# Value products four units behind instead of three, five tiles of transposed probabilities instead of four, and each group's output stored right behind its last eviction

## The chip, the core and the metric

The kernel runs on one core of a Trainium2 chip. Its engines each work through their own instructions in order and wait for one another through semaphores: TensorE (PE) multiplies, VectorE (DVE), ScalarE (ACT) and GpSimd (POOL) work on tiles, and SyncE (SP) and ScalarE issue the DMA transfers. The metric is the device time of one execution in microseconds, the median of the runs. In what follows PEld is TensorE's weight load, and "ACTq" and "SPq" are the sequencers of ScalarE and SyncE, which issue DMAs.

## The reference, cut to what matters

One layer of an encoder over 4096 tokens of width 1024. A single projection feeds two halves: a gated convolution of width 3, and attention with 8 heads of 64. Attention is a band of 64 neighbours to each side, taken three times, over tokens at distance 1, 4 and 16, and the three results are mixed by their log-sum-exp:

```python
for window, dilation in ((128, 1), (512, 4), (2048, 16)):
    logits = einsum(q, k) * dh ** -0.5 + bias        # 128 queries by 256 keys at a time
    m = max(logits); p = exp(logits - m); denom = sum(p)
    o = einsum(p, v) / denom;  lse = m + log(denom)
mix = softmax(stack(lses));  o = sum(mix * outs)
x = x + einsum(concat(y_conv, o * silu(z_attn)), w_out)
```

## The kernel before, in words

The program has three stages. The first projects every token to queries, keys, values and gate and writes them to DRAM (up to about 740 us of the profile). The second, from 740 to 1834 us, interleaves two streams of work on every engine: the attention, and the dense matmuls of the convolution half (L854 to L856, `fill`). The third, from 1834 us to the end, joins the three attention results and applies the output projection, a tile of 128 tokens at a time. The order of every engine's instructions is the order in which the Python code emits them; no scheduler moves them.

The attention is cut into 384 **units**. A unit is 128 queries by up to 256 keys for a pair of heads. Eight units with the same heads, dilation and place are a **group**, so there are 48 groups; below, b is a unit's place in its group (0 to 7). A unit u goes through these steps:

- `qk` (L1044, L1045): the logits on TensorE; `logits` (L1057): bias and row maximum on VectorE, written into a tile `L`, the maximum into the group's output tile `ot`; `exps` (L1066): the exponential on ScalarE, in place.
- `p_hi` and `p_lo`: the probabilities as two half-precision parts, by ScalarE and then VectorE. For a unit with u % 3 == 1, TensorE first transposes the probabilities (`tr_pe`, L1086), and `p_hi` (L1092) and `p_lo` (L1104) write the two parts into a tile `pt`. For the other two of three, `p_hi` (L1098) and `p_lo` (L1108) write them untransposed into one of three tiles `src`, and a DMA transposition issued by SP (`tr`, L1112) brings them into `pt`.
- `av` (L1123 to L1125): twelve small matmuls of `pt` with the values `vt`; ScalarE evicts the product into `ot` (L1126).

The loop over units (L1162 to L1209) emits, in iteration u: `p_hi(u)`, `p_lo(u)`, `exps(u+1)`, `tr(u)`, half of the iteration's dense matmuls, `av(u - LAG)`, `qk(u+2)`, `logits(u+2)`, the group's transfers, the other half of the dense matmuls, and `tr_pe(u+1)` where u+1 is of that kind. So `LAG` says how many units the value products are behind the probabilities, and `PTB`, the number of `pt` tiles, is one more than that.

The group's transfers are issued on ScalarE's queue. The store of the group before (`o_store`, L1137 to L1141: one DMA of 528 KB, or two of 264 KB where the dilation is 16) and the load of the values of the next group (`load_v`, L935 to L952: three, four or, for the first and last groups of dilation 1, eight DMAs) each have their place by b. There are two `ot` tiles, so `logits` of the first unit of a group (emitted two iterations ahead, at b = 6 of the group before) may write only when the store of the group two before has landed.

The rings of tiles share one SBUF budget. `WB` is the number of staging tiles `wst` (128 x 512 float, 2 KB a partition, as a `pt` tile) in the second and third stage. They take the bias tables, and near the end of the second stage the output weights, which ScalarE's queue loads (L138) and `split` (L131 on ScalarE, L134 on VectorE or GpSimd) cuts into two parts; each of these loads is emitted two background steps behind the split of the tile three loads before it.

Of the kernel before, what the change touches and what calls it, by code (L numbers as in the profile page):

```python
# [46 lines left out]
BIG = 3.0e38  # L47
VEC = 383
CJ = (0, 2, 3, 1)
PTB = 4  # L50
CHUNKS = ((0, 1024, 71, 1), (1024, 2048, 79, 1), (2048, 3072, 87, 1), (3072, 4096, 94, 2))
SRCB = 3
LB = 3
WA = 3
WB = 4
WD = 12
LAG = 3
QZB = 4


# [5 lines left out]
def tile_hybrid_block(  # L66
# [581 lines left out]
    phB = ExitStack()  # L648
    stage[0] = phB.enter_context(tc.tile_pool(name="stageB", bufs=WB))
    pb = phB.enter_context(tc.tile_pool(name="pb", bufs=1))  # L650
# [60 lines left out]
    def c_room4():  # L711
        M["res", 1] = pb.tile([128, 1024], F32, name="bt")
        M["ja1"] = pb.tile([128, 512], F32, name="bt0")
# [12 lines left out]
    def sz_load(t):  # L726
        nc.sync.dma_start(M["sz", t % 3], sz_d[t * 128:(t + 1) * 128])
# [39 lines left out]
    def y_planes(t):  # L767
        halves = M["ja0", t % 2].bitcast(U16).rearrange("p (c b) -> p b c", b=2)
        src = pb.tile([128, 2, 512], U16, name="L", bufs=LB)
        YA[t] = pb.tile([128, 2, 4, 128], U16, name="pt", bufs=PTB)  # L770
        nc.vector.tensor_copy(src[:, 0], halves[:, 0])
# [186 lines left out]
    for gi, (pr, g, grp) in enumerate(groups):  # L958
        d = DILS[g]
        for b in range(8):  # L960
# [8 lines left out]
            U = dict(pr=pr, g=g, d=d, grp=grp, gi=gi, b=b, vidx=vidx, kn=256, c0=0)  # L969
# [92 lines left out]
    def exps(u):  # L1062
        U = units[u]
        ot, b, L = OT[U["gi"]], U["b"], ST[u]
        for i in range(2):
            nc.scalar.activation(L[:, i], L[:, i], AF.Exp, scale=-1.0,  # L1066
                                 bias=ot[:, b, i, DH:DH + 1], accum_out=ot[:, b, i, DH + 1:DH + 2])
# [3 lines left out]
    def by_pe(u):  # L1071
        return u % 3 == 1

    def src_of(u):
        return SRC[(u - (u + 1) // 3) % SRCB]
# [12 lines left out]
    def p_hi(u):  # L1088
        U = units[u]
        if by_pe(u):  # L1090
            PT[u] = pb.tile([128, 2, 2, 2, 128], F16, name="pt", bufs=PTB)
            nc.scalar.activation(PT[u][:, 0].rearrange("p a b q -> p (a b) q"), ST[u], AF.Copy, scale=P_SCALE)  # L1092
            return
        src = src_of(u)
        c = slice(U["c0"], U["c0"] + U["kn"])
        if U["kn"] < 256:
            nc.gpsimd.memset(src.rearrange("p a b c -> p (a b) c")[:, :, dead(U)], 0.0)
        nc.scalar.activation(src[:, 0, :, c], ST[u], AF.Copy, scale=P_SCALE)  # L1098

    def p_lo(u):  # L1100
        U = units[u]
        if by_pe(u):
            hi, lo = (PT[u][:, n].rearrange("p a b q -> p (a b) q") for n in range(2))
            nc.vector.scalar_tensor_tensor(lo, ST.pop(u), P_SCALE, hi, op0=OP.mult, op1=OP.subtract)  # L1104
            return
        c = slice(U["c0"], U["c0"] + U["kn"])
        src = src_of(u)
        nc.vector.scalar_tensor_tensor(src[:, 1, :, c], ST.pop(u), P_SCALE, src[:, 0, :, c], op0=OP.mult, op1=OP.subtract)  # L1108

    def tr(u):  # L1110
        PT[u] = pb.tile([128, 2, 2, 2, 128], F16, name="pt", bufs=PTB)
        nc.sync.dma_start(PT[u].rearrange("p a b c q -> p (a b c) q"), src_of(u).rearrange("p a b c -> p (a b c)"), transpose=True)  # L1112
# [49 lines left out]
    for u in range(NU):  # L1162
        U = units[u]
        p_hi(u)
        p_lo(u)
        if u + 1 < NU:
            exps(u + 1)
        if not by_pe(u):
            tr(u)
        fill(pers[u] / 2)  # L1170
        if u >= LAG:
            av(u - LAG)
        if u + QZB + 2 < NU and units[u + QZB + 2]["d"] == 1 and units[u + QZB + 2]["b"] % 2 == 0:
            q_order(u + QZB + 2)
        if u + QZB + 1 < NU:
            q_alone(u + QZB + 1)
        if u + 6 < NU:
            k_dense(u + 6)
        if u + 2 < NU:
            qk(u + 2)  # L1180
        if u + 3 == NU:
            c_room2()
            sz_load(0)
        if u + 2 < NU:
            logits(u + 2)
        if u + 3 == NU:
            c_room4()
        if u > 8 and U["b"] == LAG + 1:
            o_store(U["gi"] - 1)
        if U["b"] == LAG and U["gi"] + 1 < len(groups):  # L1190
            VT[U["gi"] + 1] = load_v(*groups[U["gi"] + 1])
        fill(pers[u] / 2)
        if u + 1 < NU and by_pe(u + 1):
            tr_pe(u + 1)
        if state["done"]:
            for _ in range(4):
                if bg:
                    bg.pop(0)()
        pr = U["pr"]
        if u == 4:  # L1200
            load_bias(0, 0)
            load_bias(0, 1)
        for a, b, at, rate in CHUNKS:
            p, n = divmod(u - at, 96)
            for n in range(rate * n, min(5, rate * n + rate) if 0 <= p < 3 else 0):
                load_stacks(p + 1, n, a, b)
        n = u - LAG
        if n > 0 and n % 32 == 0 and n // 32 <= 9:
            load_bias((n - 32) // 96 + 1, order[0][(n // 32 - 1) % 3])  # L1209
# [7 lines left out]
    list(conv_half(2, 0))  # L1217
    for u in range(NU - LAG, NU):
        av(u)
# [97 lines left out]
```

## Time and profile before

| | |
|---|---|
| median of 3 runs | 2181.21 us |
| lowest and highest | 2176.76 and 2185.51 us |
| the profiled execution's own time | 2186.28 us |
| its span, first to last instruction | 2184.5 us |
| PE busy | 2081.3 us, 95% |
| DVE, ACT, POOL busy | 66%, 49%, 39% |
| mean granted TensorE clock | 0.987 |

The page of the profile has a line for each group of instructions, with the busy time, the mean of one, and the idle time of the engine just before them with what ended it. The view of waits gives for each pair "engine line <- what it waited for" the sum in us, the number of waits and the longest. A timeline row has the start in us, the duration, the engine, line, operation and tiles, and in brackets the idle time before it and what ended that. A row of a windows view has for each engine the busy time and in parentheses the number of instructions, then the granted TensorE clock, the busy share of the DMA engines, and what they moved in GB/s.

### The profile page before, as it was taken

What the parts mean: (1) busy time and instruction counts of PE and PEld (TensorE: products, weight loads), DVE (VectorE), ACT (ScalarE), POOL (GpSimd) and SP (SyncE); (2) the same over time, 40 slices, a digit from 0 to 9 for tenths busy, and PEclk for the clock granted to TensorE, in tenths of its full rate; (3) what the DMA queues carried; (4) which work ended last, traced back from release to release, by engine and by line L of the source; (5) the groups of instructions that cost most, each with busy time, mean ns of one, the idle gap of its engine ahead of it and who ended that gap; (6) DMA issues with size and microseconds to landing.
All of it is one profiled execution on the core that took longest, in us unless ns stands there. A gap on an engine that the chain in (4) does not pass through costs nothing. (4 is left out here: it accounts for less than half of the span.)

```text
span 2184.5 us, 48540 instructions
## 1 busy us (share of the span) xinstructions
PE 2081.3 (95%) x17462; PEld 1533.7 (70%) x17462; DVE 1441.1 (66%) x4032; ACT 1069.4 (49%) x3095; POOL 851.8 (39%) x1635
## 2 busy tenths in 40 slices
PE   7699999999999989998999999999999999999999
PEld 3244444444444778888888888888888887788887
DVE  7755666656665366766677656675667676887776
ACT  6323333433432167666677656666667674222221
POOL 0322232332323265433554346433453454343332
PEclk9899999999999999999999999999999999999999
DMA  5255489975554877799877998769977687787775
GB/s 204 88 153 174 142 176 172 221 177 161 169 169 137 179 138 164 147 164 186 164 160 137 172 194 136 153 120 176 204 141 129 122 171 225 233 256 244 244 244 183
DMA packets 692397, 378.34 MB, mean 173 GB/s; under 512 B 470721, under 2 KB 636732, under 8 KB 688060
## 3 DMA queue, kind: packets, MB, share of 16 engines
q1 hardware_dynamic: 570788, 304.72, 62.0%
q10 hardware_dynamic: 121368, 70.53, 13.7%
q8 instruction: 137, 2.24, 0.4%
q14 instruction: 104, 0.85, 0.1%
HBM read 157.77 MB, written 110.39 MB: 123 GB/s over the span
## 5 line engine op out<-in xcount | busy, mean ns | idle before, releaser
L854 PE MATMUL bank<-hb,w 128*128 128x256 f16 x2048 | 560.9, 274 | 0.3 <-ACT cu L861 0.3
L856 PE MATMUL bank<-hb,w 128*128 128x256 f16 x2048 | 560.8, 274 | 0.0
L855 PE MATMUL bank<-hb,w 128*128 128x256 f16 x2048 | 560.8, 274 | 0.0
L410 PE MATMUL bank<-wa,hb 128*128 128x512 f16 x1024 | 391.4, 382 | 14.9 <-DMA hb<-xs 11.4
L1057 DVE CUSTOM_DVE_ANT_0 L<-bank,bt,alpha 128x256 f32<-128x256 f32 (+1 forms) x768 | 319.0, 453 | 126.3 <-PE bank L1045 74.1
L1066 ACT ACTIVATE L<-L,ot 128x256 f32<-128x256 f32 (+1 forms) x768 | 364.2, 476 | 60.0 <-DVE ot L1057 58.4
L412 PE MATMUL bank<-wa,hb 128*128 128x512 f16 x1024 | 391.2, 382 | 0.8 <-DMA hb<-xs 0.7
L411 PE MATMUL bank<-wa,hb 128*128 128x512 f16 x1024 | 390.9, 382 | 0.3 <-DVE wa L301 0.2
L1018 POOL COPY qz<-qk 64x128 f16<-64x128 f16 x512 | 163.9, 320 | 152.9 <-PE bank L1045 134.6
L1108 DVE SCALAR_TENSOR_TENSOR src<-L,src 128x512 f16<-128x512 f32 (+1 forms) x256 | 171.3, 669 | 71.6 <-ACT src L1098 67.5
L856 PEld LDWEIGHTS <-w 128*128 128x128 f16 x2048 | 201.2, 98 | 24.0
L855 PEld LDWEIGHTS <-w 128*128 128x128 f16 x2048 | 201.2, 98 | 22.8 <-issue 0.5
L854 PEld LDWEIGHTS <-w 128*128 128x128 f16 x2048 | 201.3, 98 | 20.7
L238 POOL TENSOR_TENSOR rs_rq<-rs_mq,mhalf 128x8 f32<-128x8 f32 x64 | 104.9, 1639 | 268.4 <-DVE rs_mq L237 261.4
L410 PEld LDWEIGHTS <-hb 128*128 128x128 f16 x1024 | 101.6, 99 | 136.4 <-DMA hb<-xs 13.8
L1123 PE MATMUL bank<-vt,pt 128*128 128x64 f16 x1536 | 176.6, 194 | 18.9 <-DMA pt<-src 16.3
L412 PEld LDWEIGHTS <-hb 128*128 128x128 f16 x1024 | 100.6, 98 | 125.3 <-issue 4.4
L411 PEld LDWEIGHTS <-hb 128*128 128x128 f16 x1024 | 100.8, 98 | 123.5 <-issue 5.5
L1125 PE MATMUL bank<-vt,pt 128*128 128x64 f16 x1536 | 176.6, 194 | 0.0
L1124 PE MATMUL bank<-vt,pt 128*128 128x64 f16 x1536 | 176.5, 194 | 0.0
L1098 ACT ACTIVATE src<-L 128x512 f16<-128x512 f32 (+1 forms) x256 | 148.4, 580 | 52.4 <-issue 25.2
L441 ACT ACTIVATE h<-wk 128x512 f16<-128x512 f32 x64 | 40.3, 630 | 257.2 <-DVE wk L437 152.3
(211 smaller groups left out, 4440.1 us busy)
## 6 DMA issues: line engine op xcount, KB each, us to landing
o_d<-ot ACTq DMA_DIRECT2D x32, 528.0 KB, 6.1
qk<-o_d SPq DMA_DIRECT2D x63, 264.0 KB, 4.4
hT<-hb SPq DMA_DIRECT2D x16, 1024.0 KB, 4.1
wst<-in_w_in_dram SPq DMA_DIRECT2D x64, 256.0 KB, 3.2
hb<-hT SPq DMA_DIRECT2D x16, 1024.0 KB, 6.4
qk<-in_x_dram SPq DMA_DIRECT2D x32, 512.0 KB, 5.5
qk_d<-h SPq DMA_DIRECT2D x128, 96.0 KB, 2.1
vt<-v_d ACTq DMA_DIRECT2D x48, 256.0 KB, 5.8
```

The costliest lines, as they stand in the source:

```text
L410: nc.tensor.matmul(p, hi[:, kt, :], w[:, 0], start=kt == 0, stop=False)
L411: nc.tensor.matmul(p, hi[:, kt, :], w[:, 1], start=False, stop=False)
L412: nc.tensor.matmul(p, lo[:, kt, :], w[:, 0], start=False, stop=kt == KT - 1)
L854: nc.tensor.matmul(pt, w_h, hi[:, :, kt], start=kt == 0, stop=False)
L855: nc.tensor.matmul(pt, w_h, lo[:, :, kt], start=False, stop=False)
L856: nc.tensor.matmul(pt, w_l, hi[:, :, kt], start=False, stop=kt == KT - 1)
L1057: nc.vector.tensor_tensor_reduce(out=L[:, i], in0=p[i][:, 0:kn], in1=bias[:, U["b0"]:U["b0"] + kn], scale=alpha, scalar=BIG, op0=OP.add, o ...
L1066: nc.scalar.activation(L[:, i], L[:, i], AF.Exp, scale=-1.0, bias=ot[:, b, i, DH:DH + 1], accum_out=ot[:, b, i, DH + 1:DH + 2])
L1108: nc.vector.scalar_tensor_tensor(src[:, 1, :, c], ST.pop(u), P_SCALE, src[:, 0, :, c], op0=OP.mult, op1=OP.subtract)
L1123: nc.tensor.matmul(p[:, i], hi, v[:, 0:DH], start=j == 0, stop=False)
L1124: nc.tensor.matmul(p[:, i], hi, v[:, DH:], start=False, stop=False)
L1125: nc.tensor.matmul(p[:, i], lo, v[:, 0:DH], start=False, stop=j == 1)
```

## The change

Four constants and one condition. `LAG` goes from 3 to 4 and `PTB` from 4 to 5; the added `pt` tile takes the room of one staging tile, `WB` going from 4 to 3. The last `av` of a group stands in the iteration with b == LAG - 1 of the next group, which was b = 2 and is now b = 3. The store of that group stood at b == LAG + 1 (4), two iterations later; it now stands at b == LAG - 1 (3), in the same iteration as that last `av`, right behind it. `load_v`, emitted at b == LAG, moves from 3 to 4. The reload of the bias tables goes by u - LAG and so comes one unit later, too.

```diff
-PTB = 4
+PTB = 5
@@
-WB = 4
+WB = 3
 WD = 12
-LAG = 3
+LAG = 4
@@
-        if u > 8 and U["b"] == LAG + 1:
+        if u > 8 and U["b"] == LAG - 1:
             o_store(U["gi"] - 1)
         if U["b"] == LAG and U["gi"] + 1 < len(groups):
             VT[U["gi"] + 1] = load_v(*groups[U["gi"] + 1])
```

TensorE's order at the first place that differs, iteration 3 of the loop (the rows with - are those before; L854 to L856 are dense matmuls, L1123 to L1125 `av` of unit 0, of which the first three of twelve matmuls are shown):

```order
 L856 LDWEIGHTS w_6133
 L856 MATMUL bank_7137<-hb_6257,w_6133 128x256
-L1123 LDWEIGHTS pt
-L1123 MATMUL bank_7194<-vt,pt 128x64
-L1124 LDWEIGHTS pt
-L1124 MATMUL bank_7194<-vt,pt 128x64
-L1125 LDWEIGHTS pt
-L1125 MATMUL bank_7194<-vt,pt 128x64
```

The value products of unit 0 leave iteration 3 for iteration 4, at the same place in the iteration, and so on for every unit; the last four units' products stand behind the loop, where there were three.

ScalarE's order around the group's transfers, units 179 and 180 (b = 3 and 4 of the group numbered 22, of dilation 4). L1098 is `p_hi`, L1066 `exps`, L1126 the eviction of `av`, L939 to L943 `load_v`, L1139 `o_store`, L861 an eviction of the dense matmuls. Before:

```order
L1098 ACTIVATE src_6576<-L 128x512 [waits Activation_49]
L1066 ACTIVATE L,ot<-L,ot 128x256 [waits DVE_49] x2
L1126 ACTIVATE ot<-bank_16469 128x2x64 [waits PE_49]
L939 DMA vt<-v_d 64x8x256 [waits DMAHW4_49]
L940 DMA vt<-v_d 64x8x256 [waits DMAHW6_49]
L942 DMA vt<-v_d 64x256 [waits DMAHW7_49]
L943 DMA vt<-v_d 64x256 [waits DMAHW0_49]
L861 ACTIVATE cu<-bank_16440,inv 128x256 [waits PE_49]
L1098 ACTIVATE src_6574<-L 128x512 [waits Activation_49,Pool_49]
L1066 ACTIVATE L,ot<-L,ot 128x256 [waits DVE_49] x2
L1126 ACTIVATE ot<-bank_16526 128x2x64 [waits PE_49]
L1139 DMA o_d_83<-ot 128x8x132 [waits DMAHW2_49]
```

With the change:

```order
L1098 ACTIVATE src_6576<-L 128x512 [waits DMAHW3_49,Activation_49]
L1066 ACTIVATE L,ot<-L,ot 128x256 [waits DVE_49] x2
L1126 ACTIVATE ot<-bank_16455 128x2x64 [waits PE_49]
L1139 DMA o_d_83<-ot 128x8x132 [waits Activation_49]
L861 ACTIVATE cu<-bank_16426,inv 128x256 [waits PE_49]
L1098 ACTIVATE src_6574<-L 128x512 [waits DMAHW6_49,Pool_49]
L1066 ACTIVATE L,ot<-L,ot 128x256 [waits DVE_49] x2
L1126 ACTIVATE ot<-bank_16508 128x2x64 [waits PE_49]
L939 DMA vt<-v_d 64x8x256 [waits DMAHW7_49,DMAHW4_49]
L940 DMA vt<-v_d 64x8x256 [waits DMAHW0_49]
L942 DMA vt<-v_d 64x256 [waits DMAHW1_49]
L943 DMA vt<-v_d 64x256 [waits DMAHW2_49]
```

The store comes one iteration earlier and ahead of the value loads instead of behind them, and it waits for ScalarE's own eviction (Activation) right in front of it; the value loads come one iteration later.

ScalarE's order where the output weights are loaded and split, near the end of the second stage. L138 is the load of a staging tile, L131 ScalarE's part of a split. Before:

```order
L131 ACTIVATE w_26655<-wst 128x512 [waits DMAHW2_49]
L824 DMA y_d<-cc 128x257 [waits Pool_49]
L1126 ACTIVATE ot<-bank_26666 128x2x64 [waits PE_49]
L138 DMA wst<-in_w_out_dram 128x512 [waits DMAHW0_49,Activation_49]
L131 ACTIVATE w_26699<-wst 128x512 [waits DMAHW3_49]
L1092 ACTIVATE pt<-bank_26707 128x512 [waits PE_49]
```

With the change:

```order
L131 ACTIVATE w_26641<-wst 128x512 [waits DMAHW2_49]
L824 DMA y_d<-cc 128x257 [waits Pool_49]
L1126 ACTIVATE ot<-bank_26652 128x2x64 [waits PE_49]
L138 DMA wst<-in_w_out_dram 128x512 [waits DMAHW0_49,Pool_49]
L131 ACTIVATE w_26685<-wst 128x512 [waits DMAHW3_49]
L1092 ACTIVATE pt<-bank_26693 128x512 [waits PE_49]
```

The order is the same, but the load goes into the tile that the split just before it reads, so it now waits for GpSimd's part of that split (Pool), which before belonged to a tile one load further back.

## The prediction

> **What bounds the kernel now.** I read the page first, then TensorE's groups with the idle time before each, then stretches of the second stage, and last the timeline around single waits.
>
> ```profile
> span 2184.5 us, 48540 instructions
> PE 2081.3 (95%) x17462; PEld 1533.7 (70%) x17462; DVE 1441.1 (66%) x4032; ACT 1069.4 (49%) x3095; POOL 851.8 (39%) x1635
> ...
> L1123 PE MATMUL bank<-vt,pt 128*128 128x64 f16 x1536 | 176.6, 194 | 18.9 <-DMA pt<-src 16.3 <-ACT ct L866 1.6 <-ACT ot L1126 0.9
> L1086 PE MATMUL bank<-identf,L 128*128 128x128 f32 x512 | 88.2, 283 | 32.3 <-ACT L L1066 22.9 <-POOL L L1053 8.0
> ```
>
> TensorE is busy 95% of the span, and the change takes no matmul from it, so only its idle time can be won. The second stage, which alone the change touches:
>
> ```profile
> core 0: us, PE busy (x) PEld busy (x) DVE busy (x) ACT busy (x) POOL busy (x), PEclk, DMA share, GB/s
> 740.00:1834.00 1094.00, 1038.95 (x12702) 928.92 (x12699) 723.94 (x2444) 712.52 (x2450) 523.14 (x1372) 0.99 0.86 161
> ```
>
> There TensorE idles 1094.0 - 1039.0 = 55 us. Nearly all of it is in the two groups above: the value products wait 18.9 us, 16.3 of them for DMA transpositions (`pt`), and TensorE's own transpositions 32.3 us, 22.9 of them for ScalarE's exponentials. Every other unit of work on the other engines has cover: VectorE and ScalarE are busy two thirds of this stage.
>
> How late a transposition is, and why, the worst case shows (iterations 179 to 183, group 22):
>
> ```profile
> 1247.32 0.64 ACTq L939 DMA_DIRECT2D vt<-v_d  x1
> ...
> 1250.54 0.38 ACTq L1139 DMA_DIRECT2D o_d<-ot  x1
> 1252.06 11.84 SPq L1112 DMA_TRANSPOSE pt<-src  x3
> 1260.97 0.42 DVE L1057 CUSTOM_DVE_ANT_0 L<-bank,bt,alpha 128x192 f32<-128x192 f32 x1 [5.15 <-DMA o_d<-ot]
> 1261.43 0.46 ACT L1066 ACTIVATE L<-L,ot 128x192 f32<-128x192 f32 x1 [3.12 <-DVE ot L1057]
> 1261.91 0.23 PE L1123 MATMUL bank<-vt,pt 128*128 128x64 f16 x1 [2.88 <-DMA pt<-src]
> ```
>
> Value loads, the store and transpositions stand together in the DMA queues. The store, issued at 1250.5, lets VectorE go on only at 1261.0; ScalarE then waits for VectorE; and the transposition issued at 1252.1 lets the value product go only at 1261.9. The same in sums, with the time to landing of tile `ot`'s DMAs and then of the transpositions L1112:
>
> ```profile
> DVE L L1057 <- DMA o_d<-ot: 38.7, 20, 5.1
> ...
> DMA to landing us min/median/max: 2.9/5.2/10.3
> ...
> DMA to landing us min/median/max: 3.0/3.7/8.1
> ```
>
> **The change, part by part.** *Value products one unit later.* One unit takes
>
> ```profile
> L1123 PE MATMUL bank<-vt,pt x1536: 189/193/261, 770.0 to 1832.5; 128*128 128x64 f16 x192
> ```
>
> (1832.5 - 770.0) / 383 = 2.77 us. That is the slack each transposition gains, at no added instruction. The waits for `pt` in the view of waits (sum, number, longest):
>
> ```profile
> PE bank L1123 <- DMA pt<-src: 16.3, 18, 2.9
> ```
>
> None is longer than a unit by more than 0.1 us, so almost all would fit. Some lateness will grow where TensorE no longer pauses; I keep 1.5 us of the 16.3: **-14.8** (bounds -16.3 and, if half returns, -8). The two other waits before L1123 (1.6 for a dense eviction, 0.9 for ScalarE's eviction of the bank) loosen a little: **-1** (-2.5 to 0).
>
> *The granted clock.* The wait of 2.88 us has a second price:
>
> ```profile
> 1261.70:1265.10 3.40, 3.19 (x25) 2.64 (x26) 1.73 (x8) 0.99 (x5) 0.00 (x0) 0.50 0.56 110
> 1265.10:1272.00 6.90, 6.90 (x82) 6.27 (x81) 5.35 (x17) 5.32 (x18) 2.97 (x7) 1.00 1.11 250
> ```
>
> For 3.4 us behind it the clock is 0.50, so about 3.4 x 0.5 = 1.7 us of matmul time is lost: **-1.7** if this wait goes. The same stands behind another wait, the one of 3.78 us quoted below:
>
> ```profile
> 1794.20:1797.60 3.40, 3.37 (x26) 2.57 (x25) 2.80 (x7) 3.40 (x13) 2.61 (x3) 0.50 1.15 252
> ```
>
> [...]
>
> *Store earlier, loads later, both on ScalarE's queue.* The store gains one iteration (2.8 us) on the tile's next user, so of VectorE's waits for it (mean 38.7 / 20 = 1.9 us) only the few above 2.8 should leave anything. That is not on TensorE's path by itself; it keeps VectorE, and ScalarE behind it, from being late when TensorE stops pausing.
>
> What ScalarE's issuing costs TensorE shows in eight loads for a group of dilation 1:
>
> ```profile
> 1786.29 0.77 ACTq L949 DMA_DIRECT2D vt<-v_d  x1
> ...
> 1791.70 0.46 ACTq L952 DMA_DIRECT2D vt<-v_d  x1
> 1792.21 0.63 ACT L131 ACTIVATE w<-wst 128x512 fp32r<-128x512 f32 x1 [4.91 <-DMA vt<-v_d]
> 1793.90 1.18 PE L1086 MATMUL bank<-identf,L 128*128 128x128 f32 x4 [3.78 <-ACT L L1066]
> ```
>
> While the sequencer issues, `p_hi` and `exps` stand behind it, and the next transposition on TensorE waits. Which one is hit depends on the unit number modulo 3, so on the group number g modulo 3. Unit by unit from the timeline:
>
> ```profile
> 862.43 0.93 PE L1086 MATMUL bank<-identf,L 128*128 128x128 f32 x4 [0.28 <-ACT L L1066]
> 885.89 0.93 PE L1086 MATMUL bank<-identf,L 128*128 128x128 f32 x4 [0.49 <-ACT L L1066]
> 846.62 0.88 PE L1086 MATMUL bank<-identf,L 128*128 128x128 f32 x4 [1.04 <-ACT L L1066]
> 784.38 0.90 PE L1086 MATMUL bank<-identf,L 128*128 128x128 f32 x3 [5.34 <-POOL L L1053]
> ```
>
> In 12 of the 16 groups with g % 3 = 1 the unit at b = 5, two units behind the load, waits (first 862.43, last 1793.90, sum 11.3 us). With g % 3 = 2 it is b = 6 (5 waits, the first at 885.89, sum 4.1), with 0 it is b = 7 (the first after the start at 846.62; 10 waits, 7.9; the 5.34 at 784.38 is the start of the stage, behind the first bias table, and stays). Loads one unit later turn the classes: g % 3 = 2 becomes the hardest, 0 the middle, 1 the mildest. Two loads of eight, now in the hardest place (3.78 us above, 1.88 at 1724.6 below), move to the mildest, where such a load costs about 1 (846.62 follows one): -3.5. Seven loads of eight move from the mildest to the middle: about +0.5 each, +3.5. Loads of three or four exchange places: about -2. The store's own wait for its eviction costs ScalarE some tenths of a us in each group, less than the order before, where the store followed the loads at once. Sum about **-2**, bounds -8 (the mildest price everywhere) and +8.
>
> *What comes back.* After a removed pause TensorE reaches the next transposition earlier, and ScalarE's exponentials may not be there. At 1261.9 they would be, since ScalarE's lateness came from the store as well; elsewhere not always. I take **+3** (0 to +8, half of the 16.3).
>
> *Three staging tiles instead of four.* In the last 59 us of the stage:
>
> ```profile
> 1775.00:1834.00 59.00, 52.27 (x548) 43.35 (x546) 43.81 (x118) 40.24 (x125) 37.72 (x50) 0.97 0.94 228
> ...
> 1784.65 0.63 ACT L131 ACTIVATE w<-wst 128x512 fp32r<-128x512 f32 x1
> ...
> 1787.31 1.27 POOL L134 TENSOR_TENSOR w<-wst,w 128x512 fp32r<-128x512 f32 x1
> ```
>
> A load on ScalarE's queue now waits for the split just before it. GpSimd's part ended at 1788.58, 3.3 us behind ScalarE's at 1785.28; VectorE's parts follow within about 1 us. Behind the waiting load stand `p_hi` and `exps`, and TensorE's next transposition waits for those. Some eleven loads, 0.5 to 2 us each, are about 8 us of a ScalarE that has 59.0 - 40.2 = 18.8 idle; from the pair 4.91 to 3.78 above, a block of 5 us cost at most 3.8. I take **+3** (0 to +8). Bias tables use one tile at a time; the third stage uses one a token tile; both stay covered.
>
> *The ends.* One more value product moves behind the loop, where TensorE waits 3.5 us for VectorE anyway:
>
> ```profile
> 1836.28 1.08 PE L762 MATMUL bank<-identf,vt 128*128 128x128 f32 x4 [3.48 <-DVE vt L756]
> ```
>
> So that costs 0. Reloading a bias table one unit later has 64 units of room: 0.
>
> Sum: -14.8 - 1.0 - 1.7 - 2 + 3 + 3 = **-13.5 us**. The profiled execution, 2186.28 us (its span and 1.8 us around it), becomes 2172.8. It lies 5.1 us above the median of the runs, so the median becomes 2181.2 - 13.5 = **2168 us**.
>
> **The rivals.**
>
> *A, the pauses change place.* TensorE's waits for `pt` go, but its transpositions take them over, since ScalarE's queue sets the pace behind each group's transfers. For it: 32.3 us of waits already stand there, twice those for `pt`; `src` has only three tiles, so `p_hi` of every third unit still needs the transposition of four units before, and a late one now holds ScalarE instead. Against: ScalarE is idle a third of the stage. Then the +3 for what comes back becomes +11 and the shift of classes 0: -13.5 + 8 + 2 = -3.5, **2178 us**. [...]
>
> *B, more is won.* VectorE no longer stalls 38.7 us for stores, so the exponentials come earlier too, and the remaining slow-clock stretches go: all of 16.3, 2.5, 8 of the transpositions' waits, 1.7, one more slow stretch (1.7), +3 at the staging tiles: -16.3 - 2.5 - 8 - 1.7 - 1.7 + 3 = -27, **2154 us**.
>
> *C, slower.* Store and loads, in neighbouring iterations as before but with the store's wait for the eviction, block ScalarE twice, and the eight-DMA loads must wait for the store's landing, which is now seven or eight DMAs back on the same semaphores. Today those waits sum to about 25 us (11.3 + 4.1 + 7.9 and 1.7 outside the classes), 25 / 47 = 0.5 us for each group with a load. The gains are 14.8 + 1 + 1.7 = 17.5. The rival decides when the mean wait passes (25 + 17.5 + 11) / 47 = 1.1 us. At 1.2 us the waits are 56: +31 - 17.5 = +13.5, **2195 us**; at the 1.88 us of one such wait they would be 88, and the loss 46 us.
>
> ```profile
> 1724.60 0.93 PE L1086 MATMUL bank<-identf,L 128*128 128x128 f32 x4 [1.88 <-ACT L L1066]
> ```
>
> Against it: by then the store has had 2.8 us and six issues of 0.5 to 0.8 us, more than its median landing of 5.2 us.
>
> That the change doesn't do what it says is excluded by the order: the value products do stand one unit later.
>
> **How the numbers follow.** Forecast 0.60, A 0.23, B 0.09, C 0.08. 0.5% (about 11 us) is what a measurement of this kernel tells from no change. The forecast's own range, 2161 to 2178 from its bounds, has two thirds below 2170: 0.40 faster, 0.20 same. A is same; B faster; C slower, but for 0.01 that stays within. With 0.02 of A on the faster side, faster 0.40 + 0.09 + 0.02 = 0.51, same 0.42, slower 0.07. The range holds A and most of B: **2155 to 2183**.
>
> **What would show it.** In the profile of the changed kernel: waits of L1123 for `pt` below 3 us in all; VectorE's wait for `o_d` below 10 instead of 38.7; TensorE's transpositions between 25 and 35; no slow clock at the place of 1261.7; L138 on ScalarE's queue followed by idle time on ScalarE between 1775 and 1830. If L1086's waits rise above 40, A; if they pass 60, C. The prediction fails if transpositions land more than a unit later than now, or if the loads' new class is dear.

## The result, and the profile after

The changed kernel takes 2197.61 us (median of nine runs, 2188.33 to 2201.77) against 2181.21 (nine runs of the kernel before beside it): ratio 1.0070, 95% interval 1.0053 to 1.0088. It is **slower by 0.7%**, some 15 us, and lies outside the predicted range of 2155 to 2183. Its profiled execution, 2194.21 us, is one of the faster of the nine.

The page and the groups of the changed kernel that answer to those shown of before:

```profile
span 2192.4 us, 48505 instructions
PE 2083.4 (95%) x17462; PEld 1535.1 (70%) x17462; DVE 1444.2 (66%) x4032; ACT 1068.7 (49%) x3095; POOL 851.1 (39%) x1635
...
L1123 PE MATMUL bank<-vt,pt 128*128 128x64 f16 x1536 | 176.4, 194 | 10.3 <-ACT ot L1126 6.4 <-DMA pt<-src 3.8
...
L1086 PE MATMUL bank<-identf,L 128*128 128x128 f32 x512 | 89.5, 286 | 46.2 <-ACT L L1066 39.2 <-POOL L L1053 5.7
```

TensorE's wait ahead of the value products fell from 18.9 to 10.3 us, as intended; ahead of its own transpositions it rose from 32.3 to 46.2. The second stage, and where the last value product stands (before: 1832.5):

```profile
core 0: us, PE busy (x) PEld busy (x) DVE busy (x) ACT busy (x) POOL busy (x), PEclk, DMA share, GB/s
740.00:1847.00 1107.00, 1044.54 (x12710) 933.67 (x12708) 729.11 (x2446) 712.02 (x2450) 522.27 (x1372) 0.98 0.86 159
847.60:854.40 6.80, 6.17 (x39) 4.71 (x40) 5.21 (x19) 4.61 (x17) 2.76 (x6) 0.52 0.86 231
```

```profile
L1123 PE MATMUL bank<-vt,pt x1536: 189/193/261, 773.0 to 1845.3; 128*128 128x64 f16 x192
```

The stage ends 12.8 us later. TensorE idles 1107.0 - 1044.5 = 62.5 us in it instead of 55, and more of the stage runs at half clock: the stretch at 847.6 is one of eight. Summed over the profile's clock records, the stage holds 20.5 us at 0.50 before and 37.5 after, so the loss, half of that, goes from 10.2 to 18.8 us. (One more stretch of before, 6.8 us at 1835.1, stands just behind the stage; over the whole executions the loss goes from 28.9 to 33.6 us.) The view of waits of the changed kernel:

```profile
engine line waited for: us in total, times, longest us
...
DVE src L1108 <- ACT src L1098: 100.8, 82, 5.5
...
PE bank L1086 <- ACT L L1066: 39.2, 28, 4.0
...
POOL bt L921 <- DMA wst<-bv_d: 31.8, 4, 10.6
...
PE bank L1123 <- DMA pt<-src: 3.8, 4, 1.5
```

And one row of the kernel before that the prediction did not look at:

```profile
POOL bt L921 <- DMA wst<-bv_d: 17.0, 4, 6.0
```

VectorE's wait for the store (`o_d`, 38.7 us before) has gone from the list, the waits for `pt` are 3.8 instead of 16.3, and GpSimd's wait for a bias table in its staging tile has nearly doubled. This last row is what the experiments lead to.

### The profile page after: what moved, and what is told of

Same layout as the page of the kernel before. It is cut to its first block, busy times and chain, and to the rows that moved or that the text cites. A ratio compares the mean times of both kernels' runs of the same rounds, so it can differ in the third digit from the quotient of the medians.

```text
span 2192.4 us, 48505 instructions
## 1 busy us (share of the span) xinstructions
PE 2083.4 (95%) x17462; PEld 1535.1 (70%) x17462; DVE 1444.2 (66%) x4032; ACT 1068.7 (49%) x3095; POOL 851.1 (39%) x1635
## 3 DMA queue, kind: packets, MB, share of 16 engines
q10 hardware_dynamic: 121368, 70.53, 13.9%
## 5 line engine op out<-in xcount | busy, mean ns | idle before, releaser
L854 PE MATMUL bank<-hb,w 128*128 128x256 f16 x2048 | 562.8, 275 | 0.2 <-ACT cu L861 0.2
L856 PE MATMUL bank<-hb,w 128*128 128x256 f16 x2048 | 562.3, 275 | 0.0
L410 PE MATMUL bank<-wa,hb 128*128 128x512 f16 x1024 | 390.9, 382 | 14.6 <-DMA hb<-xs 10.9
L1066 ACT ACTIVATE L<-L,ot 128x256 f32<-128x256 f32 (+1 forms) x768 | 363.6, 476 | 32.8 <-DVE ot L1057 31.4
L856 PEld LDWEIGHTS <-w 128*128 128x128 f16 x2048 | 202.0, 99 | 24.8
L854 PEld LDWEIGHTS <-w 128*128 128x128 f16 x2048 | 202.1, 99 | 21.4
L1098 ACT ACTIVATE src<-L 128x512 f16<-128x512 f32 (+1 forms) x256 | 148.5, 580 | 104.3 <-issue 36.3
L1123 PE MATMUL bank<-vt,pt 128*128 128x64 f16 x1536 | 176.4, 194 | 10.3 <-ACT ot L1126 6.4
L1125 PE MATMUL bank<-vt,pt 128*128 128x64 f16 x1536 | 176.4, 194 | 0.0
```

What stands on the lines that cost most here:

```text
L410: nc.tensor.matmul(p, hi[:, kt, :], w[:, 0], start=kt == 0, stop=False)
L854: nc.tensor.matmul(pt, w_h, hi[:, :, kt], start=kt == 0, stop=False)
L856: nc.tensor.matmul(pt, w_l, hi[:, :, kt], start=False, stop=kt == KT - 1)
L1066: nc.scalar.activation(L[:, i], L[:, i], AF.Exp, scale=-1.0, bias=ot[:, b, i, DH:DH + 1], accum_out=ot[:, b, i, DH + 1:DH + 2])
L1123: nc.tensor.matmul(p[:, i], hi, v[:, 0:DH], start=j == 0, stop=False)
L1125: nc.tensor.matmul(p[:, i], lo, v[:, 0:DH], start=False, stop=j == 1)
```

## The experiments

The reasons to be told apart, by the letters that the expectations use. P: the loads' place at b = 4 is dear. L: the later value products are dear by themselves. S: the store right behind its eviction holds ScalarE. W: three staging tiles are dear. B: the later reload of the bias tables is. Each ratio is to the kernel before on the same chip, with its 95% interval.

### First round: the parts of the change

**Later products with the transfers in their old iterations.** From the changed kernel:

```diff
-        if u > 8 and U["b"] == LAG - 1:
+        if u > 8 and U["b"] == 4:
             o_store(U["gi"] - 1)
-        if U["b"] == LAG and U["gi"] + 1 < len(groups):
+        if U["b"] == 3 and U["gi"] + 1 < len(groups):
```

> The changed kernel (value products four units behind, five tiles of transposed probabilities, three staging tiles) with the transfers in the iterations of the kernel before: loads of V at b = 3, store at b = 4. Theory P (the loads' place: at b = 4 ScalarE's issuing hits TensorE's transpositions of the groups g % 3 = 0, whose waits rose to 29 us): those waits fall back to about 13 us, the waits for pt stay near 4, and the time is 2168 to 2178 us. Theory L (the later value products themselves: where TensorE no longer pauses for pt it pauses for the exponentials): the sum of L1086's waits stays at 42 to 50 us and the time at 2190 to 2202 us. Theory S (store right behind its eviction): since the store is not there any more, as P, 2168 to 2180. Theory W (three staging tiles): 2190 to 2200, with the loss behind 1775 us alone.

Measured: 2206.73 us, 1.0080 (1.0051 to 1.0109). P loses its case: with the old places the loss is the same. So does S, for this kernel has no store behind its eviction. The run is not a clean test of the places, since VectorE's waits for the store are back in it (45.4 us) and L1086's waits are 58.4 us, more than L had; the next run is.

**The new places with the products three units behind.** From the kernel before, `o_store` at b = 3 and `load_v` at b = 4 (LAG, PTB and WB stay).

> The kernel before (value products three units behind, four tiles of transposed probabilities, four staging tiles) with the transfers in the changed kernel's iterations: store at b = 3, loads of V at b = 4. Theory P: slower than before, since the loads now hit the transpositions of g % 3 = 0 and the 16 us of waits for pt stay as well: 2190 to 2205 us, L1086's waits 42 to 50 us. Theory L: as before, 2177 to 2186 us, L1086's waits 30 to 36 us. Theory S: between, some tenths of a us per group, 2180 to 2195, and only where ScalarE's evictions L1126 stand ahead of the store. Theory W: as before, 2177 to 2186.

Measured: 2183.03 us, 0.9988 (0.9972 to 1.0004). L1086's waits are 22.0 us, where P had 42 to 50. The places cost nothing, and P falls.

**Three staging tiles alone.** From the kernel before, `WB = 3`.

> The kernel before with three staging tiles for the weights of the third stage instead of four, and nothing else. Theories P, L and S: as before, 2177 to 2187 us (my term in the prediction was +3). Theory W: 2190 to 2200 us, with TensorE's busy time between 1775 and 1834 us below the 52.3 us of before by 5 or more.

Measured: 2190.92 us, 1.0013 (0.9996 to 1.0031): W is at most a small part. One thing more is to be learned here. This kernel does what the kernel before does until the output weights are split near 1790 us, and yet its profiled execution falls some 8 us behind that of before between the first unit and unit 104 (from the start times of the scores' products). A single profile cannot carry a difference of 8 us; the ratios of repeated runs can.

**The store one iteration behind the loads.** From the changed kernel, `o_store` at `LAG + 1`, so b = 5.

> The changed kernel with the store at b = 5, behind the loads (b = 4), as in the kernel before it stood one iteration behind them; the value products stay four units behind. Theory P: the loads stay where they hurt: 2190 to 2205 us, VectorE's waits for o_d come back in part (20 to 40 us), L1086's waits 42 us or more. Theory S: without the store ahead of the loads and behind its eviction it is 2168 to 2180 us. Theories L and W: as the changed kernel, 2188 to 2202.

Measured: 2234.76 us, 1.0228 (1.0198 to 1.0259), worse than any theory had it. Its view of waits shows the price of a late store:

```profile
DVE L L1057 <- DMA o_d<-ot: 102.2, 31, 6.0
...
PE bank L1086 <- ACT L L1066: 63.2, 37, 6.0
```

`ot` has two buffers and the next group's first scores are written at b = 6, so a store at b = 5 leaves one iteration for its landing. With products four units behind the store may not come that late; one at b = 4 (the first run above, 1.0080) cannot be told from the change's b = 3.

**The store right behind its eviction in the kernel before.** `o_store` at `LAG - 1` = 2, `load_v` at 3, LAG 3.

> The kernel before with the store right behind the group's last eviction and ahead of the loads (store at b = 2, loads at b = 3), value products three units behind as before. Theory S (a store that stands behind its own eviction and ahead of the loads holds ScalarE): slower than before by 0.3% or more, with the idle time before L1098 up as it was in the changed kernel (52 to 104 us). Theory L (only the later value products cost): not slower, ratio 0.996 to 1.000, VectorE's waits for o_d from 38.7 to below 5 us and L1086's waits at or below the 32 us of before.

Measured: 2223.04 us, 1.0156 (1.0131 to 1.0182). Slow, as S had it, but not where S had it: in its waits stand

```profile
ACT pt L1092 <- DMA vt<-v_d: 30.9, 5, 7.9
...
PE bank L1123 <- DMA pt<-src: 22.3, 23, 3.2
```

ScalarE's `p_hi` stands behind loads that wait for other transfers. In the longest of these waits, 7.9 us up to 1391.36, the seventh of eight loads waits for the store's second half to land (1387.82) and the eighth for a transposition (1390.98), each by a semaphore that the two transfers share. The changed kernel has its store just as close to the eviction, one iteration later, and without the moved reload (below) it is level with the kernel before, so the store's own wait is not the price. Why the same order one iteration earlier costs 1.6% in all was not settled.

### Second round: the reload, and the lag alone

**The bias reloads back in unit 3.** From the changed kernel:

```diff
-        n = u - LAG
+        n = u - 3
         if n > 0 and n % 32 == 0 and n // 32 <= 9:
```

> The changed kernel with the reloads of the bias tables back in the iteration in which the kernel before has them (unit 3 of a group and not 4, where the loads of V now stand); all else as changed. Theory B (bias reload and loads of V in one iteration collide: GpSimd's wait for bv_d rose from 17 to 32 us): that wait falls back to about 17 us and the ratio to before goes from 1.007 to 1.003 or less. Theory L: ratio 1.005 to 1.009, whatever that wait does; it is ten iterations of 384.

Measured: 2191.18 us, 1.0016 (0.9998 to 1.0034).

**Products back at three units**, all else as changed (`LAG = 3`; store at b = 3 and loads at b = 4 written as numbers; the reloads follow LAG).

> The changed kernel (five tiles of transposed probabilities, three staging tiles, store at b = 3, loads of V at b = 4) with the value products back at three units behind (the bias reloads, which follow them, with them). Theory L: the loss goes with the products: ratio to before 0.998 to 1.003 (the 0.13% of three staging tiles less the 0.12% that the places won), L1123's waits for pt at about 20 us and L1086's for exponentials at 15 to 25. If it stays at 1.005 or more, the cause is in the tiles' number or their places in memory, and L falls.

Measured: 2187.46 us, 0.9994 (0.9978 to 1.0010). Both undo the loss. They share one thing, the reload in unit 3. So the changed kernel itself was run again beside the variant with early reloads, on one chip:

> The changed kernel once more, unaltered, beside its variants on the same chip, because its ratio of 1.007 came from other runs of the kernel before (median 2181.2, against 2187.7 beside the later experiments). Theory B (the bias reloads' iteration costs what lies between 1.0016 and 1.007): 1.005 to 1.009 again, and at least 0.3% above the variant with early reloads. If it comes to 1.000 to 1.004, B falls: the reloads cost nothing that can be measured, and the loss depends on which chip runs it.

> The changed kernel with the reloads of the bias tables in unit 3 of a group, once more, beside the unaltered changed kernel. Theory B: 1.000 to 1.003, at least 0.3% below the changed kernel. Without an effect of the reloads: the same ratio as the changed kernel within 0.25%.

Measured: changed 2203.74 us, **1.0062** (1.0041 to 1.0082); with early reloads 2190.66 us, **1.0008** (0.9993 to 1.0024). B stands: of the loss of 0.6 to 0.7%, 0.54 points, some 12 us, hang on a reload that happens nine times in 384 iterations, three of them through a staging tile.

What is left of the change is the lag: 1.0008 with four units, 0.9994 with three. The waits for `pt` that went bought nothing that can be measured. Products three units behind:

```profile
L1123 PE MATMUL bank<-vt,pt 128*128 128x64 f16 x1536 | 176.6, 194 | 24.7 <-DMA pt<-src 21.1 <-ACT ot L1126 2.5 <-ACT cu L861 0.4
...
L1086 PE MATMUL bank<-identf,L 128*128 128x128 f32 x512 | 86.1, 282 | 29.8 <-ACT L L1066 23.3 <-POOL L L1053 5.4
```

Four units behind, early reloads:

```profile
L1123 PE MATMUL bank<-vt,pt 128*128 128x64 f16 x1536 | 176.2, 194 | 7.9 <-ACT ot L1126 5.2 <-DMA pt<-src 2.6
...
L1086 PE MATMUL bank<-identf,L 128*128 128x128 f32 x512 | 89.0, 285 | 40.6 <-ACT L L1066 34.3 <-POOL L L1053 5.2
```

The waits for `pt` fall by 18.5 us; 10.8 come back at L1086, and 2.7 ahead of L1123 itself, for ScalarE's evictions. The slow clock takes a little more: summed over its records, the stage loses 13.7 us with three units and 15.4 with four. The 3 us or so that would be left are not seen in the ratios, which differ by 0.14 points the other way (by 0.22 between the first run with early reloads, 1.0016, and that with three units, on one chip), within their intervals.

**The value product right ahead of TensorE's transposition.** In the changed kernel, `av(u - LAG)` moves from ahead of the scores to behind the second `fill`, and store and loads behind it.

> The changed kernel with the value product of an iteration (still four units behind) moved from ahead of the next scores' products to right ahead of TensorE's own transposition; eviction, store and loads follow it in the same order as now. Theory L, in the form that TensorE has spent its cover when it comes to the transposition: 0.7 us of value products now stand between the scores and the transposition, and the scores reach VectorE 0.7 us earlier, so each of the 28 waits for exponentials shortens by up to 1.4 us: L1086's waits from 46 to 15 to 25 us, the ratio to before 0.995 to 1.001. If L1086's waits stay above 40 us, what holds ScalarE is longer than that cover or follows TensorE's own pace, and the time stays at 1.004 to 1.010. The evictions, held by later products, could also hold p_hi: then ScalarE's idle time before L1126 rises, and the time with it.

Measured: 2222.43 us, 1.0159 (1.0134 to 1.0184). The idea of cover falls: L1086's waits are 66.4 us and not 15 to 25. The evictions are the reason, as the last sentence had it:

```profile
DVE src L1108 <- ACT src L1098: 194.8, 170, 5.5
...
ACT ot L1126 <- PE bank L1125: 156.3, 230, 2.4
```

In the changed kernel the second of these is

```profile
ACT ot L1126 <- PE bank L1125: 36.5, 75, 4.2
```

ScalarE waits 156 us for products that come late, and `p_hi` and all that follows stand behind.

### How one unit costs 12 us

A reload of the table of dilation 1 goes through a staging tile and is copied by GpSimd. SP's order around it, before (the units of the transpositions are 66, 68 and 69):

```
L1112 DMA_TRANSPOSE pt<-src_6576
L917 DMA wst<-bv_d 128x256 x2
L1112 DMA_TRANSPOSE pt<-src_6574
L1112 DMA_TRANSPOSE pt<-src_6575
```

and with the change:

```
L1112 DMA_TRANSPOSE pt<-src_6576
L1112 DMA_TRANSPOSE pt<-src_6574
L917 DMA wst<-bv_d 128x256 x2
L1112 DMA_TRANSPOSE pt<-src_6575
```

Unit 67 is transposed by TensorE, so a reload in its iteration has no transposition ahead of it on SP; unit 68 has one, which waits for VectorE's `p_lo`. The same holds for the other two (163 and 164, 259 and 260). GpSimd waits for none of that and is at its copies at once. The changed kernel, GpSimd, SP, ScalarE and TensorE from their timelines (start, duration):

```profile
942.81 7.79 SPq L1112 DMA_TRANSPOSE pt<-src  x3
...
947.22 0.64 POOL L1018 COPY qz<-qk 64x128 f16<-64x128 f16 x2 [1.54 <-PE bank L1045]
...
950.66 1.09 SPq L917 DMA_DIRECT2D wst<-bv_d  x2
...
956.74 1.89 POOL L921 COPY bt<-wst 128x128 f32<-128x128 f32 x4 [8.88 <-DMA wst<-bv_d]
...
962.33 0.31 POOL L1097 MEMSET src<- 128x256 f16 x1
...
962.66 1.23 SPq L1112 DMA_TRANSPOSE pt<-src  x1
...
969.91 1.25 SPq L1112 DMA_TRANSPOSE pt<-src  x1
...
974.59 0.64 ACTq L942 DMA_DIRECT2D vt<-v_d  x1
978.49 0.49 ACTq L943 DMA_DIRECT2D vt<-v_d  x1
979.08 0.63 ACT L1098 ACTIVATE src<-L 128x512 f16<-128x512 f32 x1 [5.61 <-DMA pt<-src]
...
982.22 0.33 PE L1086 MATMUL bank<-identf,L 128*128 128x128 f32 x1 [1.87 <-ACT L L1066]
```

The chain can be followed up to the clock. GpSimd stands for 8.88 us. So its memset of `src` for unit 71 comes at 962.33, and unit 71's transposition is issued at 962.66 (its `p_hi` began at 956.2). SP then issues without a pause, and unit 74's goes out at 969.91 and lands at 978.5. The fourth value load of the group waits, by the program's semaphores, for the landing of that transposition: it is issued at 978.49, and ScalarE has stood 5.61 us when it comes to the `p_hi` behind it. TensorE's transposition of unit 79 then waits 1.87 us, and the clock drops to 0.50 for 3.4 us from 984 on.

The same stretch with early reloads, first its row of waits, then its timeline:

```profile
POOL bt L921 <- DMA wst<-bv_d: 14.6, 5, 4.2
```

```profile
944.05 1.05 SPq L917 DMA_DIRECT2D wst<-bv_d  x2
...
947.74 1.47 POOL L921 COPY bt<-wst 128x128 f32<-128x128 f32 x4 [4.20 <-DMA wst<-bv_d]
...
972.49 0.64 ACTq L942 DMA_DIRECT2D vt<-v_d  x1
973.17 0.61 ACTq L943 DMA_DIRECT2D vt<-v_d  x1
973.88 0.63 ACT L1098 ACTIVATE src<-L 128x512 f16<-128x512 f32 x1 [2.40 <-issue]
```

Unit 74's transposition lands at 968.6, the four loads follow each other without a gap, ScalarE stands 2.40 us, and unit 79 waits 0.2 us in all. One link stays open: that transposition takes 3.8 us to land here (issued at 964.78) and 8.6 in the changed kernel, and what made it slower is not shown. The wait of 1.87 us stands in the second profile of the changed kernel too (1.88), and in neither of the two with early reloads. From unit 72 to 88 the changed kernel loses 5.3 us on the other in the means of two profiles each (5.2 to 5.5 in each of the four pairs), from 168 to 184 5.9 (4.8 to 6.9), from 256 to 272 3.0 (2.3 to 3.7): the stretches at the three reloads, 14 us together, as much as the whole loop differs (13.7).

Is it SP's queue (Q), a collision with the loads of V in the same iteration (C), or any later place (N)? Two more places for the reload, `n = u - 6` and `n = u - 5` in the changed kernel:

> The changed kernel with the bias reloads in unit 6 of a group (units 70, 166, 262, transposed by TensorE; on SP's queue behind the transposition of the unit before). Theory Q (the reload stands behind the transposition of its own iteration on SP, while GpSimd, which has no such wait ahead, already stands at the copies): GpSimd arrives one iteration (2.8 us) later at a reload that is issued no later, its wait for bv_d is 3 to 6 us each, and the ratio to before 1.000 to 1.003. Theory C (collision with the loads of V of the same iteration): the same. Theory N (any place later than unit 3 is dear): 1.005 to 1.008.

> The changed kernel with the bias reloads in unit 5 of a group (units 69, 165, 261, transposed by DMA; on SP's queue in the same place as with unit 6). Theory Q: GpSimd stands at the copies while SP still waits for the transposition ahead: waits of 8 to 11 us, ratio 1.005 to 1.008, as the changed kernel. Theory C: no load of V stands in this iteration, waits of 3 to 5 us and 1.000 to 1.003. Theory N: 1.005 to 1.008.

Measured: unit 6 2197.61 us, 1.0038 (1.0021 to 1.0055); unit 5 2202.26 us, 1.0061 (1.0039 to 1.0083). GpSimd's waits, for unit 6:

```profile
POOL bt L921 <- DMA wst<-bv_d: 21.9, 4, 7.2
```

and for unit 5:

```profile
POOL bt L921 <- DMA wst<-bv_d: 29.9, 4, 10.1
```

In unit 5 no loads of V stand in the iteration, and the price is the whole: C falls. Units 5 and 6 have the same place on SP's queue, but GpSimd comes an iteration later with 6, waits less, and the price is half. The waits of 14.6 (unit 3), 21.9 and 29.9 us go with ratios of 1.0008, 1.0038 and 1.0061. That is Q, though unit 6 came out dearer than Q had it. Its interval reaches up to N's 1.005, so what speaks against N is this order and the chain above more than the one ratio.

**The moved reload alone**, in the kernel before (`n = u - 4`):

> The kernel before with the bias reloads in unit 4 of a group instead of 3, and nothing else. Theory Q: GpSimd's waits for bv_d go from 3.2 to 6.0 us each to 8 to 11, and the ratio is 1.004 to 1.008, the price that the changed kernel pays. If the products three units behind hide it (TensorE waits for pt at those places anyway): 1.000 to 1.003.

Measured: 2194.69 us, 1.0037 (1.0024 to 1.0050), with

```profile
POOL bt L921 <- DMA wst<-bv_d: 30.3, 4, 10.4
```

So this edit alone costs 8 us. It is 0.54 points in the changed kernel and 0.37 here. The intervals are too wide to tell the two apart, so that a part is hidden where TensorE still waits for `pt` is not shown.

### Third round: is ScalarE's issuing the limit?

If the pauses return at L1086 because ScalarE stands while it issues three to eight loads, the loads should be spread. `load_v` here only lists its transfers, and the loop issues two an iteration:

```diff
-        if u > 8 and U["b"] == LAG + 1:
+        if u > 8 and U["b"] == 3:
             o_store(U["gi"] - 1)
-        if U["b"] == LAG and U["gi"] + 1 < len(groups):
-            VT[U["gi"] + 1] = load_v(*groups[U["gi"] + 1])
+        if U["b"] == 4 and U["gi"] + 1 < len(groups):
+            VT[U["gi"] + 1], loads = load_v(*groups[U["gi"] + 1])
+        run_tasks(loads, 2)
```

Once in the kernel before, and once in the changed kernel with early reloads:

> The kernel before (products three units behind, four tiles of transposed probabilities, four staging tiles) with the store at b = 3 and the loads of V two at a time, from b = 4 to at most b = 7, instead of three to eight at once. Theory I (ScalarE stands still while it issues: 160 us in all for the loads of before, 4.5 to 6.0 us for each eight, and TensorE's transposition behind pays): each stop is at most about 2 us, L1086's waits fall from 22.9 for the exponentials to below 15, no wait behind an eight, and the ratio is 0.990 to 0.997. Against I: where ScalarE waits for the same landing or the same DMA queue, two at a time wait as long, and the ratio is 0.998 to 1.002, as with the loads at b = 4 at once (0.9988).

> The changed kernel with the loads of V two at a time from b = 4 on and the bias reloads in unit 3; products four units behind. Theory I: what the later products only moved to L1086 (34.9 us in the variant with early reloads) falls below 20, and since the waits for pt stay near 2 us, the ratio is 0.986 to 0.994, below that of the same loads with products three units behind. Theory A (the pauses only change place, whatever stands on ScalarE's queue): 0.998 to 1.004, not below the other.

Measured: three units behind 2155.47 us, 0.9848 (0.9825 to 0.9871); four units behind 2139.89 us, 0.9773 (0.9749 to 0.9796). The same loads at once stood at 0.9988 and 1.0008. TensorE's transpositions (L1086 has become L1091) with three units, then with four:

```profile
L1091 PE MATMUL bank<-identf,L 128*128 128x128 f32 x512 | 80.8, 278 | 8.6 <-ACT L L1071 4.5 <-POOL L L1058 3.8
```

```profile
L1091 PE MATMUL bank<-identf,L 128*128 128x128 f32 x512 | 82.5, 278 | 20.8 <-ACT L L1071 15.5 <-POOL L L1058 4.8
```

In the trace of before, the loads of V take 139 us in all from a group's first issue to the end of its last, 4.1 to 5.9 us for each eight. I stands, by more than it had forecast, and A falls: with ScalarE freed, the later products are worth 0.75 points. That transpositions might land sooner where fewer loads stand beside them is not the reason: the median landing that the profiles tell is 4.5 us with the loads at once and three units behind and 4.5 two at a time, 4.4 and 4.7 with four.

**Two at a time with the late reload** (`n = u - LAG`):

> Products four units behind, loads of V two at a time from b = 4, and the bias reloads in unit 4 as in the changed kernel. If GpSimd's wait is the price whatever ScalarE does (Q): waits of 8 to 11 us again and 0.981 to 0.984, 0.4 to 0.6% above the same with early reloads (0.9773). If it costs only where ScalarE is late too: 0.976 to 0.979.

Measured: 2154.86 us, 0.9845 (0.9822 to 0.9867): 0.7 points above the same with early reloads. The late reload eats the whole gain of the later products here.

**Thinner still**, `run_tasks(loads, 1 + (len(loads) > 7 - U["b"]))`: one transfer an iteration, two while more are left than iterations to b = 7 (so eight go two by two, four as 2, 1, 1). Four units behind, then three:

> Products four units behind, bias reloads in unit 3, and the loads of V one an iteration from b = 4 on (two where eight must be out by b = 7). If ScalarE's stops for issuing were still a limit at two an iteration: L1086's waits from 15.5 for the exponentials to below 10 and 0.972 to 0.976. If what is left comes from the transposition's landing and GpSimd: 0.976 to 0.979.

> Loads of V one an iteration (two while more are left than iterations to b = 7), store at b = 3, reloads in unit 3, but products three units behind, four tiles of transposed probabilities and four staging tiles. If the later products are worth the waits for pt once ScalarE is free: 0.979 to 0.984, 0.5 to 1% above the same with products four units behind (0.9735), with 17 to 25 us of waits for pt. If the thinner issue alone is the gain: 0.973 to 0.976.

Measured: four units 2129.92 us, **0.9735** (0.9714 to 0.9755); three units 2147.04 us, 0.9835 (0.9816 to 0.9854). The first is the fastest of all, some 58 us below the kernel before. Its rows for the two waits (L1123 and L1086 have become L1128 and L1091):

```profile
L1128 PE MATMUL bank<-vt,pt 128*128 128x64 f16 x1536 | 175.1, 193 | 6.5 <-DMA pt<-src 6.5
...
L1091 PE MATMUL bank<-identf,L 128*128 128x128 f32 x512 | 80.4, 276 | 10.4 <-ACT L L1071 5.9 <-POOL L L1058 4.1
```

and those of three units behind:

```profile
L1128 PE MATMUL bank<-vt,pt 128*128 128x64 f16 x1536 | 175.6, 193 | 21.3 <-DMA pt<-src 21.1 <-ACT ot L1131 0.2
...
L1091 PE MATMUL bank<-identf,L 128*128 128x128 f32 x512 | 78.9, 274 | 8.0 <-POOL L L1058 4.4 <-ACT L L1071 3.4
```

Here 14.8 us leave the first row and 2.4 come back in the second. Not every microsecond of the gain is placed: with two loads an iteration and three units behind, TensorE's busy time itself is 2067.4 us instead of 2081.3. Of these 13.9 us 7.4 stand at its transpositions (88.2 to 80.8), and the slow clock explains about 1.4 us.

## Why the prediction was wrong, point by point

**Two steps failed. The first is "Reloading a bias table one unit later has 64 units of room: 0".** It looked at when the table is next read. It did not ask what the reload's transfers are moved past on SP's queue, a transposition that waits for `p_lo`, nor who waits for them at once, GpSimd with its copies. The runs put this step at 8 us alone and 12 us within the change, most of the loss. The forecast and the result are some 29 us apart (-13.5 and +15): this step is 12 of them, and without it the change would still have come out at 1.0008, some 15 us above the forecast.

**Value products one unit later, -14.8.** The waits for `pt` went as said (16.3 to 3.8; forecast 1.5). The gain did not come.

**The second is "What comes back", +3 (0 to +8).** It is the term that was mis-sized: with early reloads 10.8 us came back at L1086, 2.7 at the evictions ahead of L1123 and 1.7 to the clock, 15.2 of 18.5. The sentence that most of it would not return rested on one place, 1261.9. Rival A had the mechanism, and its mark, L1086 above 40, was met (46.2, and 40.6 with early reloads). With loads of one an iteration 2.4 came back: +3 holds only for a kernel that does not stop ScalarE for each group's loads. That L1123's waits fell by 14.8 us there, as the first term says, is luck: it is another kernel, whose waits for `pt` start from 21.1 us, and its time fell by 1.0 points, more than these waits.

**The granted clock, -1.7.** The slow stretch at 1261.7 went, but eight stand in the stage instead of six, and three of them last 6.8 us: 18.8 us lost instead of 10.2. Wrong in sign. The term counted the wait that went and not the new waits.

**Store earlier, loads later, -2 (-8 to +8).** The places came out at 0.9988, some -2.6 us, within the bounds. The rule by unit number modulo 3 did not hold: groups with g % 3 = 0, forecast middle, hold about 29 of the 46.2 us of the changed kernel, those with 2, forecast hardest, 11.5. With three units and the same places L1086 waits 22.0 us in the kernel before and 29.8 in the changed one, no more than before (32.3), so the places alone are not what raised it.

**Three staging tiles, +3.** 1.0013 (0.9996 to 1.0031): right in size, and not told from nothing.

**Rival C** had 2195 us and the sign by luck: its cause, store and loads that block ScalarE more than before, is not what the change cost, for without the moved reload the changed order stands at 1.0008 in all. Loads that hold ScalarE do cost time, as the third round shows, but they did so before the change as well.

**The range.** Said to come from the bounds of the terms, 2161 to 2178 us is narrower than they are: added up they reach from -28.5 to +14.3 us, 2153 to 2196.

## What to carry to other kernels

A constant that shifts one stage may shift others that are written in its terms; list every transfer that moves with it, what it passes on its queue, and who stands waiting at once, not only when its data are next needed. A wait removed from the bounding engine is worth what the next wait on it leaves: measure that wait's own cause first. Here three to eight transfers issued in a row on the engine that also computes were that cause, and issuing one or two an iteration turned a lag worth nothing that could be measured into one worth 0.75 to 1%.

## What was not expected of the hardware

In the changed kernel's profile short waits of TensorE go with a slower clock, but not each: of its twelve waits over 1.8 us in the stage, eight (among them 1.87, 2.21 and 2.29 us) have a stretch of 3.4 or 6.8 us at 0.50 beside or behind them, and four (1.82, 2.78, 3.27 and 3.57 us) have none. So the length of a wait does not tell them apart.

What does can be read from the clock records of the kernel before and of the changed one. In each, the slow stretches of the stage start whole multiples of 3.413 us apart (before, 1261.7 - 783.8 = 477.9 us is 140 of them; changed, 1250.1 - 782.5 = 467.6 us is 137). Divide the changed kernel's stage at these steps and add up TensorE's idle time in each piece: the eight pieces ahead of slow stretches idle 2.07 to 3.37 us, and no other piece at full clock idles more than 1.97. The wait of 3.57 us fell into two pieces, which idle 1.95 and 1.63 us, and cost no clock; that of 1.87 fell into one, which with shorter pauses idles 2.15. In the kernel before, the six pieces ahead of slow stretches idle 1.71 to 3.41 us, and no other at full clock more than 1.65. So in each of the two profiles the idle time added up in a piece parts the waits that cost clock from those that did not, though not at one value: a piece of 1.71 us has half clock behind it in the one, and one of 1.97 us has not in the other. How the clock is granted is not shown.

In the changed kernel's profile an issue on ScalarE's queue stands behind the landing of a transposition of SP's, by the program's shared semaphores: from the third value load's issue to the fourth's it is 3.9 us (974.59 to 978.49). With early reloads, where the transposition has landed before, it is 0.7 us (972.49 to 973.17).
